# Weights in rings of fixed places, wide low parts and sums, and high products first, in a one-core transformer block

## The chip, the cores and the metric

The kernel runs on one core of a Trainium2 chip. The metric is the device time of one execution in microseconds. The time before is the median of three runs, and one more execution of the same program was profiled.

A core has a matrix engine (TensorE, PE in the profile; its loads of the stationary operand are shown apart as PEld), a vector engine (VectorE, DVE), a scalar engine (ScalarE, ACT), GpSimd (POOL), and a queue engine (SyncE, SP) that here issues most transfers. Each has its own queue of instructions. Data lie in SBUF, sums of products in PSUM, which here is used as eight banks of 128 rows by 512 float32 columns.

## The reference

One layer of a streaming encoder block, for 256 tokens (two blocks of 128 rows, `h` = 0 and 1 below) and a width of 4096, in float32:

```python
xn = rms_norm(h, norm_in_g[i])
proj = xn @ w_in[i]                       # 4096 x 14336
q, k, v, z_a, a_c, g_c, z_c = jnp.split(proj, ...)
y_a = chunked_attention(q, k, v, rel_table[i])
y_a = rms_norm(y_a, attn_out_g[i]) * silu(z_a)
y_c = conv_module(a_c, g_c, w_dw[i], b_dw[i], conv_ln_g[i], conv_ln_b[i], w_pw[i], b_pw[i])
y_c = rms_norm(y_c, conv_out_g[i]) * silu(z_c)
h = h + concatenate([y_a, y_c]) @ w_out[i]                    # 4096 x 4096
gate = sigmoid(rms_norm(h, ple_norm_g[i]) @ w_ple_gate[i] + b_ple_gate[i])   # 4096 x 4096
h = h + gate * (p[i] @ w_ple[i])
return rms_norm(h, final_g)
```

`conv_module` is a gated product, a causal depthwise convolution of 31 taps, a layer norm, a swish and a product with a 2048 x 2048 matrix (`w_pw`). Nearly all the arithmetic is in the products with the five weight matrices, each of which is read about once.

## The kernel before

**Products from high and low parts.** Each operand is split in two: a high part, rounded to the format in which TensorE multiplies fast (`F32R`), and a low part, which is what the rounding left. A product of two operands is three products of parts, called kinds: kind 0 is high left with high weight, kind 1 low left with high weight, kind 2 high left with low weight. The left operand (the activations, transposed) is the stationary one; the weights stream past it, 512 columns at a time. For a weight tile `wt`, `parts_of` (L199) writes the high part with a cast on ScalarE (L204) and the low part with a subtraction on VectorE (L205).

**Mixed products.** `mixed_product` (from L340) computes two blocks of 512 output columns for both row blocks: four sums, `c[h][j]`, in four PSUM banks of the pool `ps_acc`, which has just four. It goes through the contraction in pairs of row blocks of 128, in a given order (`dense`, `early` and so on, L329 to L338). An unmarked pair is a plain pair: for each of its two weight tiles of 128 x 1024 (`k` = 0 and 1), four banks by three kinds, 24 products (`add_plain`, L395). The banks have names: P2 is `c[0][0]`, P3 is `c[0][1]`, P4 is `c[1][0]`, X is `c[1][1]`. A pair marked `*` or `+` uses seven block products of three kinds in place of eight, 21 products, with sums of weight blocks (`ua`, `ub`) and four further banks P1, P5, P6 and P7 (`helper`, from `ps_tmp`). For `*` VectorE makes the sums (L465, L466, L472, L473); for `+` two of them are made by an accumulating transfer (`sums_ahead`, L404). Of the w0 tile only the first half needs parts in a seven.

**After a product.** When a mixed product is complete, its caller reads the four banks on VectorE, in the order of `QUARTERS`: c00, c10, c01, c11. These are called drains below: L535 in `scaled_pair`, L1028 and L1030 for the pointwise convolution, L1054 in `gated`, L1138 for `w_out`, L1180 for the gate. The next mixed product allocates the same four banks.

**Where the tiles lie.** Weight tiles come from the pool `wpool` with a buffer count for each tag: five for raw tiles (`w`), three each for high and low parts (`wh`, `wl`). The parts of the sums (`uh`, `ul`) have two each in `upool`. A new tile takes a buffer when all that touched the tile in it before are done.

**Order.** Instructions are traced in program order; a scheduler then fills each engine's queue, and can put an instruction that is ready ahead of an earlier one that isn't. `pin` keeps instructions in program order; it is used in the first pairs (`first_pairs`) and at the very end. `fill` takes small pieces of other work from the deque `later` (convolution taps, transposes' splits, gating) and issues them between pairs. `queued_behind` puts the sums' parts of a `+` pair behind the last recorded part instructions (`recent`).

**Stages.** Four gated products with the convolution (`glu_conv`), four for queries and keys (`keys`), one mixed product for values and two single ones (`single_values`, through `product`), attention after each group, two pointwise products, four for the gates z, four for `w_out`, four for the final gate with the embedding's products (`product` with `ps_tmp`). The last gate product holds three pairs back (`left`) and ends with pinned instructions.

The lines that the change touches: the pool (L73), the first tiles (L107), `weight_parts` and `part_tiles` (L187 to L197), `parts_of`, `add_plain`'s use in the loop (L432 to L450), the sums `ua` (L464 to L466) and the order of the seven (L482 to L488).

Of the kernel before, what the change touches and what calls it, by code (L numbers as in the profile page):

```python
# [10 lines left out]
F32 = mybir.dt.float32  # L11
# [14 lines left out]
def hybrid_block(  # L26
# [41 lines left out]
    def pool(name, bufs, stack=ctx, side=0, **kw):  # L68
        return stack.enter_context(tc.tile_pool(name=name, bufs=bufs, side=sides[side], **kw))

    cpool = pool("cpool", 1)
    act = pool("act", 8)
    wpool = pool("wpool", 5)  # L73
    big = pool("big", 8)
    keep = pool("keep", 1)
    ps_acc = pool("ps_acc", 4, space=bass.MemoryType.PSUM)
# [27 lines left out]
            ap=[list(rows.ap[0]), [apart, 2], [1, NB]],  # L104
        )

    w_first = [wpool.tile([P, 2, NB], F32, tag="w", name="wt") for _ in range(2)]  # L107
    for j, col in enumerate((o_a, o_g)):
        nc.scalar.dma_start(w_first[0][:, j], w_in0[:P, col : col + NB])
    for lo, hi in ((0, P), (P, 2 * P), (2 * P, NB)):  # L110
# [75 lines left out]

    def weight_parts(w, col, k0, kc, tiles=None):  # L187

        wt = wpool.tile([P, KC, NB], F32, tag="w", name="wt")
        nc.sync.dma_start(  # L190
            wt[:, :kc, :],
            w[k0 * P : (k0 + kc) * P, col : col + NB].rearrange("(k q) n -> q k n", q=P),
        )
        return parts_of(wt, kc, tiles)[0]

    def part_tiles():
        return [wpool.tile([P, KC, NB], F32R, tag=tag, name=tag, bufs=3) for tag in ("wh", "wl")]  # L197

    def parts_of(wt, kc, tiles=None):  # L199
        if tiles is None:  # L200
            tiles = part_tiles()
        wh, wl = tiles
        made = (
            nc.scalar.copy(wh[:, :kc, :], wt[:, :kc, :]),  # L204
            nc.vector.tensor_tensor(  # L205
                wl[:, :kc, :], wt[:, :kc, :], wh[:, :kc, :].bitcast(F32), ALU.subtract
            ),
        )
        recent[:] = made
        return (wh, wl), made  # L210

    recent = []

# [126 lines left out]
    def mixed_product(  # L340
# [54 lines left out]
        def add_plain(n, k, wh, wl, **kw):  # L395
            pair = order[n][0]
            for j in range(2):
                for h in range(NH):
                    name = (("P2", "P3"), ("P4", "X"))[h][j]
                    add(name, block(2 * pair + k, h), (wh[:, j], wl[:, j]), n, k == 1, **kw)  # L400

        sums = {}

        def sums_ahead(n):  # L404
# [22 lines left out]
        for n, (pair, seven) in enumerate(order):  # L427
            if n < done:
                continue
            if ahead:  # L430
                ahead(pair)
            wts = []  # L432
            for k in range(2):
                wt = wpool.tile([P, 2, NB], F32, tag="w", name="wt")
                if seven == "+" and k == 0:
                    nc.sync.dma_start(wt[:, 0], w[2 * pair * P : (2 * pair + 1) * P, col : col + NB])
                else:
                    nc.sync.dma_start(wt, two_columns(w, 2 * pair + k, col, apart))
                wts.append(wt)
            sums_ahead(n)  # L440
            if n >= len(order) - n_left:
                for k in range(2):
                    tiles = left[2 * (n - len(order) + n_left) + k]
                    held.append((2 * pair + k, parts_of(wts[k], 2, tiles and tiles())[0]))
                fill(fills[n % len(fills)])
                continue
            if not seven:
                for k in range(2):
                    add_plain(n, k, *parts_of(wts[k], 2)[0])
                fill(fills[n % len(fills)])  # L450
                continue
            begins = not helper
            if begins:
                for name in ("P1", "P5", "P7", "P6"):
                    helper[name] = ps_tmp.tile([P, NB], F32, tag="tmp", name=f"acc_{name}")
                banks.update(helper)
            w0, w1 = wts
            plus = partial(nc.vector.tensor_tensor, op=ALU.add)
            before = list(recent)
            w0h, w0l = parts_of(w0, 1)[0]  # L460
            if seven == "+":
                ua = ub = sums[n]
            else:
                ua = ub = upool.tile([P, 2, NB], F32, tag="u", name="ua")  # L464
                plus(ua[:, 0], w0[:, 0], w0[:, 1])  # L465
                plus(ua[:, 1], w0[:, 1], w1[:, 1])  # L466
            with queued_behind(before if seven == "+" else ()):
                uah, ual = pair_parts(ua)
            w1h, w1l = parts_of(w1, 2)[0]
            if seven == "*" and not sums:  # L470
                ub = upool.tile([P, 2, NB], F32, tag="u", name="ub")
            plus(ub[:, 0], ua[:, 0], w1[:, 1])  # L472
            plus(ub[:, 1], ub[:, 0], w1[:, 0])  # L473
            ubh, ubl = pair_parts(ub)
            first = len(made)

            def s_of(i):
                t, at = comb[pair] if isinstance(comb, dict) else (comb[pair // 4], pair % 4)
                return [t[:, at + i // 2, q, (i % 2) * P : (i % 2 + 1) * P] for q in range(2)]

            k0, k1 = 2 * pair, 2 * pair + 1
            add("P1", block(k0, 0), (w0h[:, 0], w0l[:, 0]), n, True)  # L482
            add("P5", s_of(1), (uah[:, 0], ual[:, 0]), n, True)
            add("P7", s_of(0), (uah[:, 1], ual[:, 1]), n, True)
            add("P2", block(k1, 0), (w1h[:, 0], w1l[:, 0]), n, True)
            add("P3", s_of(3), (w1h[:, 1], w1l[:, 1]), n, True)
            add("P6", s_of(2), (ubh[:, 0], ubl[:, 0]), n, True)
            add("P4", block(k1, 1), (ubh[:, 1], ubl[:, 1]), n, True)  # L488
            if begins and on_begin:
                on_begin()  # L490
            if begins:
                tc.add_manual_dep(
                    made[first].ins, last_transpose[0].ins.name,
                    mybir.DependencyInfo(mybir.DependencyClass.NoSync, mybir.DependencyReason.DATA),
                    reason="transposes before the helpers take their banks",
                )
            if n == last_seven:
                on_helpers(helper)
            fill(fills[n % len(fills)])
# [77 lines left out]
    def first_pairs(add):  # L577
# [5 lines left out]
        def load(n):  # L583

            weights.append([])
            for k in range(2):
                t = wpool.tile([P, 2, NB], F32, tag="w", name="wt")
                pin(nc.sync.dma_start(t, two_columns(w_in0, 2 * first[n][0] + k, o_a, o_g - o_a)))
                weights[n].append(t)
            if n < n_x:  # L590
                t = act.tile([P, NH, NB], F32, tag="act", name="xin")
                src = x[0, :, n * NB : (n + 1) * NB].rearrange("(h q) n -> q h n", q=P)
                pin(nc.sync.dma_start(t, src))
                xin.append(t)
# [625 lines left out]
    fill(len(later))  # L1220
    w_p = []
    for j in range(2):
        wt = wpool.tile([P, 2, NB], F32, tag="w", name="wt")
        nc.sync.dma_start(
            wt, w_ple[0, :, (c0 + j) * NB : (c0 + j + 1) * NB].rearrange("(k q) n -> q k n", q=P)
        )
        w_p.append(pair_parts(wt))
# [111 lines left out]
```

## Time and profile before

| | |
|---|---|
| median of 3 runs | 2034.01 us (2033.57 to 2034.16) |
| the profiled execution | 2032.83 us |
| span of its instructions | 2031.1 us |
| granted TensorE clock, mean | 0.998 |
| busy: PE, PEld, DVE, ACT | 99%, 82%, 92%, 59% |
| read from HBM | 430.77 MB, 214 GB/s over the span |

The profile gives, for each engine, the time in which it worked and, for idle time, which other instruction ended it. `L205` is line 205 of the kernel; a helper's line stands for all its callers, so rows are told apart by the names of the tiles. A row of the timeline is the start, the time from the first start to the last end of a run of like instructions, and their number. A matmul's own duration (0.39 us for 512 columns) is longer than the distance to the next one, since they overlap in the array.

### The profile page before, as it was taken

To read this page: it belongs to the slowest core of one execution; us is meant where nothing else is said; L and a number is where in the kernel's file an instruction comes from. 1 tells how busy PE (TensorE), PEld (TensorE's weight loads), DVE (VectorE), ACT (ScalarE), POOL (GpSimd) and SP (SyncE) were. 2 spreads that over 40 slices of the span, in tenths; PEclk is the share of its full clock that TensorE was granted. 3 is DMA by queue.
4 is the path that set the end of the run, shared out by engine and by line. 5 is a ranking of instruction groups with operands and counts; after the bars stand their busy time and mean duration, and the time that the engine had idled before them with its cause. 6 is when DMAs were issued, how large, how long until landed. Compare 5 with 4: busy or idle time off the path is not lost.

```text
span 2031.1 us, 26144 instructions
## 1 busy us (share of the span) xinstructions
PE 2015.5 (99%) x9094; PEld 1658.7 (82%) x9094; DVE 1871.1 (92%) x2658; ACT 1203.3 (59%) x1568; POOL 46.0 (2%) x50
## 2 busy tenths in 40 slices
PE   9999999999999999999999999999999999999997
PEld 7888888888888888888888888888888888888876
DVE  7999999679999986868899999999999999999998
ACT  7655555655655445676556566675665666665555
POOL 0000000000000000000000000000000000000000
PEclk9999999999999999999999999999999999999999
DMA  8787878688678867556666666676666656666765
GB/s 294 223 237 233 257 214 251 191 245 239 188 217 250 254 187 207 171 185 205 194 214 198 202 205 214 217 229 209 206 213 201 208 187 207 204 220 205 234 208 179
DMA packets 171167, 436.69 MB, mean 215 GB/s; under 512 B 13966, under 2 KB 17182, under 8 KB 171034
## 3 DMA queue, kind: packets, MB, share of 16 engines
q1 hardware_dynamic: 161952, 417.93, 64.0%
q0 software_dynamic: 8432, 16.25, 4.9%
q8 instruction: 71, 1.16, 0.2%
q10 hardware_dynamic: 650, 0.84, 0.1%
q14 instruction: 62, 0.51, 0.1%
HBM read 430.77 MB, written 4.19 MB: 214 GB/s over the span
## 4 chain that ended last, share of the span: by engine, by line
PE 92%; DVE 5%; issue 2%; ACT 1%; DMA 1%; POOLq 0%; POOL 0%; ACTq 0%; DVEq 0%
PE acc L383 67%; PE acc_P L383 16%; PE acc L229 5%; DVE wl L205 2%; PE tmp_ps L170 1%; DVE cv L721 1%; DMA wt<-in_w_out_dram 0%; PE tmp_ps L890 0%; DVE ul L205 0%; PE tmp_ps L874 0%; PE tmp_ps L908 0%; PE tmp_ps L913 0%; ACT wh L204 0%; PE acc L371 0%; DVE cv L799 0%
## 5 line engine op out<-in xcount | busy, mean ns | idle before, releaser
L383 PE MATMUL acc<-wh,big_t 128*128 128x512 f32 x3992 | 1234.7, 391 | 0.7 <-DVE y_c L1030 0.3
L204 ACT CAST wh<-wt 128x1024 fp32r<-128x1024 f32 (+1 forms) x737 | 713.4, 978 | 550.5 <-PE acc L383 365.0
L205 DVE TENSOR_TENSOR wl<-wt,wh 128x1024 fp32r<-128x1024 f32 (+1 forms) x737 | 821.8, 1127 | 82.0 <-ACT wh L204 78.6
L383 PEld LDWEIGHTS acc<-wh,big_t 128*128 128x128 f32 x3992 | 746.8, 188 | 155.1 <-issue 0.9
L383 PE MATMUL acc<-wl,big_t 128*128 128x512 f32 x1996 | 770.7, 391 | 0.6 <-DVE wl L205 0.5
L383 PEld LDWEIGHTS acc<-wl,big_t 128*128 128x128 f32 x1996 | 374.3, 188 | 79.5 <-DVE wl L205 2.3
L204 ACT CAST uh<-ua 128x1024 fp32r<-128x1024 f32 x160 | 168.3, 1052 | 80.9 <-DVE ua L466 46.1
L721 DVE SCALAR_TENSOR_TENSOR cv<-uT,dw,cv 128x250 f32<-128x250 f32 (+19 forms) x480 | 202.3, 463 | 1.1
L205 DVE TENSOR_TENSOR ul<-ua,uh 128x1024 fp32r<-128x1024 f32 x160 | 194.9, 1218 | 8.4 <-ACT uh L204 8.0
L383 PE MATMUL acc_P<-uh,big_t 128*128 128x512 f32 x516 | 157.9, 391 | 0.0
L204 ACT CAST uh<-ub 128x1024 fp32r<-128x1024 f32 x92 | 96.8, 1053 | 95.8 <-DVE ub L473 86.5
L205 DVE TENSOR_TENSOR ul<-ub,uh 128x1024 fp32r<-128x1024 f32 x92 | 112.2, 1220 | 6.1 <-ACT uh L204 5.2
L383 PEld LDWEIGHTS acc_P<-uh,big_t 128*128 128x128 f32 x516 | 95.8, 188 | 22.3 <-ACT uh L204 3.1
L383 PE MATMUL acc_P<-ul,big_t 128*128 128x512 f32 x258 | 98.8, 391 | 0.1
L229 PE MATMUL acc<-wh,big_t 128*128 128x512 f32 x304 | 93.9, 390 | 0.0
L465 DVE TENSOR_TENSOR ua<-wt 128x512 f32<-128x512 f32 x95 | 65.1, 685 | 18.3 <-DMA wt<-in_w_in_dram 12.4
L383 PE MATMUL acc<-uh,big_t 128*128 128x512 f32 x252 | 78.1, 390 | 0.0
L383 PE MATMUL acc_P<-wh,big_t 128*128 128x512 f32 x252 | 77.8, 389 | 0.0
L229 PEld LDWEIGHTS acc<-wh,big_t 128*128 128x128 f32 x304 | 56.9, 188 | 11.9 <-issue 0.2
L383 PE MATMUL acc_P<-uh,comb_t 128*128 128x512 f32 x216 | 66.4, 390 | 0.1
L466 DVE TENSOR_TENSOR ua<-wt 128x512 f32<-128x512 f32 x95 | 64.9, 683 | 1.1 <-DMA wt<-in_w_in_dram 1.1
L473 DVE TENSOR_TENSOR ub<-ub,wt 128x512 f32<-128x512 f32 x92 | 63.0, 685 | 0.8
(250 smaller groups left out, 1589.3 us busy)
## 6 DMA issues: line engine op xcount, KB each, us to landing
wt<-in_w_in_dram SPq DMA_DIRECT2D x416, 512.0 KB, 4.5
wt<-in_w_out_dram SPq DMA_DIRECT2D x128, 512.0 KB, 4.3
wt<-in_w_ple_gate_dram SPq DMA_DIRECT2D x128, 512.0 KB, 4.2
wt<-in_w_pw_dram SPq DMA_DIRECT2D x32, 512.0 KB, 4.7
ua<-in_w_in_dram SPq DMA_DIRECT2D x31, 512.0 KB, 4.2
ua<-in_w_in_dram POOLq DMA_DIRECT2D x31, 512.0 KB, 8.3
wt<-in_w_in_dram SPq DMA_DIRECT2D x31, 256.0 KB, 2.7
hc<-in_x_dram SPq DMA_DIRECT2D x8, 512.0 KB, 4.8
```

The costliest lines, as they stand in the source:

```text
L170: nc.tensor.transpose(pt[:, i * T + h * P : i * T + (h + 1) * P], src[:, h, b] if len(src.shape) == 4 else src[:, h, b * P : (b + 1) * P], ...
L204: nc.scalar.copy(wh[:, :kc, :], wt[:, :kc, :]),
L205: nc.vector.tensor_tensor(wl[:, :kc, :], wt[:, :kc, :], wh[:, :kc, :].bitcast(F32), ALU.subtract),
L229: nc.tensor.matmul(acc, a, b[:, k, :], start=kb == 0 and kind == 0, stop=kb == kblocks - 1 and kind == 2,)
L383: nc.tensor.matmul(banks[name], a, b, start=name not in begun, stop=final and ends[name] == n and kind == 2 and not (left and name in "P2 ...
L465: plus(ua[:, 0], w0[:, 0], w0[:, 1])
L466: plus(ua[:, 1], w0[:, 1], w1[:, 1])
L473: plus(ub[:, 1], ub[:, 0], w1[:, 0])
L721: nc.vector.scalar_tensor_tensor(cv[:, i, PAD - k :], uT[:, i, : T + k - PAD], dw[:, b, k : k + 1], cv[:, i, PAD - k :], ALU.mult, ALU.add,)
```

## The change

Raw weight tiles and their parts no longer come from pool buffers but from three tiles that hold them all: five raw places, three high and three low. A counter hands out places in turn. Since the two tiles of a plain pair now lie in one tile, a strided view takes both (`places`; where the ring wraps, its step is negative), and one VectorE instruction of 128 x 2048 writes both low parts, after two casts. In a seven whose sums VectorE makes, `ua`'s two halves come from one instruction: w0's first half and w1's second half, each plus w0's second half, which is read twice by a broadcast view. In a plain pair, kinds 0 and 1 of both tiles go first, then kind 2 of both; the bank changes faster than the left operand does. In a seven, kinds 0 and 1 of the products with raw blocks, then those with `ua`, then kind 2 of each, then P6 and P4 as before. Orders, fills, casts, transfers and the number of products stay the same.

```diff
-    wpool = pool("wpool", 5)
+    wpool = pool("wpool", 1)
...
-    w_first = [wpool.tile([P, 2, NB], F32, tag="w", name="wt") for _ in range(2)]
+    RAW, PARTS = 5, 3
+    w_ring = wpool.tile([P, RAW, 2, NB], F32, name="wt")
+    wh_ring, wl_ring = (wpool.tile([P, PARTS, 2, NB], F32R, name=name) for name in ("wh", "wl"))
+    taken = {RAW: 0, PARTS: 0}
+
+    def place(n):
+
+        taken[n] += 1
+        return (taken[n] - 1) % n
+
+    def raw_place():
+        return w_ring[:, place(RAW)]
+
+    def places(n, of):
+
+        return slice(of[0], of[-1] + 1) if of[-1] > of[0] else slice(of[0], None, of[-1] - of[0])
+
+    w_first = [raw_place() for _ in range(2)]
...
     def part_tiles():
-        return [wpool.tile([P, KC, NB], F32R, tag=tag, name=tag, bufs=3) for tag in ("wh", "wl")]
+        at = place(PARTS)
+        return wh_ring[:, at], wl_ring[:, at]
...
+    def parts_of_pair(raw):
+
+        at = [place(PARTS) for _ in range(2)]
+        halves = [(wh_ring[:, i], wl_ring[:, i]) for i in at]
+        casts = [nc.scalar.copy(wh, w_ring[:, i]) for (wh, _), i in zip(halves, raw)]
+        src, to = places(RAW, raw), places(PARTS, at)
+        low = nc.vector.tensor_tensor(
+            wl_ring[:, to].rearrange("q k j n -> q k (j n)"),
+            w_ring[:, src].rearrange("q k j n -> q k (j n)"),
+            wh_ring[:, to].rearrange("q k j n -> q k (j n)").bitcast(F32), ALU.subtract,
+        )
+        recent[:] = *casts, low
+        return halves
...
+        def add_pair(n, parts):
+
+            pair = order[n][0]
+            for kinds in ((0, 1), (2,)):
+                for k, (wh, wl) in enumerate(parts):
+                    for h in range(NH):
+                        for kind in kinds:
+                            for j in range(2):
+                                name = (("P2", "P3"), ("P4", "X"))[h][j]
+                                add(name, block(2 * pair + k, h), (wh[:, j], wl[:, j]), n, k == 1, (kind,))
...
             if not seven:
-                for k in range(2):
-                    add_plain(n, k, *parts_of(wts[k], 2)[0])
+                add_pair(n, parts_of_pair(raw_at))
...
-                plus(ua[:, 0], w0[:, 0], w0[:, 1])
-                plus(ua[:, 1], w0[:, 1], w1[:, 1])
+                blocks = w_ring.rearrange("q k j n -> q (k j) n")
+                a, d = 2 * raw_at[0], 2 * raw_at[1] + 1
+                plus(
+                    ua, blocks[:, a : d + 1 : d - a] if d > a else blocks[:, a : d - 1 if d else None : d - a],
+                    blocks[:, a + 1 : a + 2].broadcast_to([P, 2, NB]),
+                )
...
-            add("P1", block(k0, 0), (w0h[:, 0], w0l[:, 0]), n, True)
-            add("P5", s_of(1), (uah[:, 0], ual[:, 0]), n, True)
-            add("P7", s_of(0), (uah[:, 1], ual[:, 1]), n, True)
-            add("P2", block(k1, 0), (w1h[:, 0], w1l[:, 0]), n, True)
-            add("P3", s_of(3), (w1h[:, 1], w1l[:, 1]), n, True)
+            raw = (
+                ("P1", block(k0, 0), (w0h[:, 0], w0l[:, 0])),
+                ("P2", block(k1, 0), (w1h[:, 0], w1l[:, 0])),
+                ("P3", s_of(3), (w1h[:, 1], w1l[:, 1])),
+            )
+            two = (
+                ("P5", s_of(1), (uah[:, 0], ual[:, 0])),
+                ("P7", s_of(0), (uah[:, 1], ual[:, 1])),
+            )
+            for group, kinds in ((raw, (0, 1)), (two, (0, 1)), (raw, (2,)), (two, (2,))):
+                for product_of in group:
+                    add(*product_of, n, True, kinds)
             add("P6", s_of(2), (ubh[:, 0], ubl[:, 0]), n, True)
             add("P4", block(k1, 1), (ubh[:, 1], ubl[:, 1]), n, True)
```

More of the change, by code (lines that the diff above doesn't have):

```diff
@@ L187, in weight_parts @@
     def weight_parts(w, col, k0, kc, tiles=None):
-        wt = wpool.tile([P, KC, NB], F32, tag="w", name="wt")
+        wt = raw_place()
         nc.sync.dma_start(
@@ L431, in mixed_product @@
                 ahead(pair)
-            wts = []
+            wts, raw_at = [], []
             for k in range(2):
-                wt = wpool.tile([P, 2, NB], F32, tag="w", name="wt")
+                raw_at.append(place(RAW))
+                wt = w_ring[:, raw_at[k]]
                 if seven == "+" and k == 0:
@@ L586, in load @@
             for k in range(2):
-                t = wpool.tile([P, 2, NB], F32, tag="w", name="wt")
+                t = raw_place()
                 pin(nc.sync.dma_start(t, two_columns(w_in0, 2 * first[n][0] + k, o_a, o_g - o_a)))
@@ L1222, in hybrid_block @@
     for j in range(2):
-        wt = wpool.tile([P, 2, NB], F32, tag="w", name="wt")
+        wt = raw_place()
         nc.sync.dma_start(
```

## The prediction

> **What bounds the kernel now.** I read the page first (busy times, the chain of waits), then the busy time by stretch, then the longest pieces of the chain, and last the timeline where one product ends and the next begins.
>
> ```profile
> span 2031.1 us, 26144 instructions
> PE 2015.5 (99%) x9094; PEld 1658.7 (82%) x9094; DVE 1871.1 (92%) x2658; ACT 1203.3 (59%) x1568; POOL 46.0 (2%) x50
> PE 92%; DVE 5%; issue 2%; ACT 1%; DMA 1%; POOLq 0%; POOL 0%; ACTq 0%; DVEq 0%
> ```
>
> In the view by stretch the columns are the stretch, its length, then busy time of PE, PEld, DVE, ACT and POOL, the granted clock, and DMA:
>
> ```profile
> 1143.00:1225.00 82.00, 82.00 (x363) 67.70 (x362) 78.31 (x94) 49.33 (x55) 0.00 (x0) 1.00 0.64 206
> 2000.00:2031.00 31.00, 18.44 (x97) 15.82 (x97) 21.90 (x40) 12.96 (x25) 1.86 (x2) 0.87 0.44 160
> ```
>
> TensorE is idle for 2031.1 - 2015.5 = 15.6 us, and 31.00 - 18.44 = 12.6 of these lie in the last stretch, where the output is scaled and stored. That leaves 3.0 us of visible idle time in the 2000 us before. A busy matmul here means one in the pipe, so I also take the spacing from two unbroken pieces of the chain:
>
> ```profile
> 713.29 43.57 PE acc L229 x192
> 1143.11 17.17 PE acc L383 x75
> ```
>
> 43.57 / 192 = 0.2269 us for one product. (17.17 / 75 gives 0.2289, with one or two short breaks in it.) A plain pair of row blocks is 24 products, 24 x 0.2269 = 5.4 us; a pair in the seven-product form is 21, 4.8 us. TensorE runs at this spacing nearly everywhere. The change issues no fewer products, so work saved on VectorE is worth at most the few stalls that are left, while each new stall is paid in full.
>
> **VectorE's saving, off the path.** Two low parts of 1024 columns become one of 2048, in plain pairs; two sums of 512 become one of 1024, in sevens whose sums are not fetched by DMA.
>
> ```profile
> L205 DVE TENSOR_TENSOR wl<-wt,wh 128x1024 fp32r<-128x1024 f32 x611 | 738.2, 1218 | 82.0 <-ACT wh L204 78.6 <-PE tmp_ps L170 1.5
> L465 DVE TENSOR_TENSOR ua<-wt 128x512 f32<-128x512 f32 x95 | 65.1, 685 | 18.3 <-DMA wt<-in_w_in_dram 12.4 <-DMA wt<-in_w_out_dram 4.4 <-DMA wt<-in_w_ple_gate_dram 1.2
> ```
>
> Of the 611 low parts 126 belong to sevens (one per seven; the orders have 126), 32 to the two single value products, 16 to the pinned start, 6 to the embedding and 3 to the end: 428 are left, 214 plain pairs. The sums give 95 sevens. What one instruction fewer saves is read from starts, since neighbours overlap:
>
> ```profile
> 1083.91 0.68 DVE L465 TENSOR_TENSOR ua<-wt 128x512 f32<-128x512 f32 x1
> 1084.51 0.68 DVE L466 TENSOR_TENSOR ua<-wt 128x512 f32<-128x512 f32 x1
> ...
> 1090.45 2.35 DVE L205 TENSOR_TENSOR wl<-wt,wh 128x1024 fp32r<-128x1024 f32 x2
> 1092.72 0.68 DVE L466 TENSOR_TENSOR ua<-wt 128x512 f32<-128x512 f32 x1
> ```
>
> 512 columns take 0.60 from start to start, 1024 take (1092.72 - 1090.45) / 2 = 1.135; the fixed part is 2 x 0.60 - 1.135 = 0.065 us, so the wide low part should take 2 x 1.135 - 0.065 = 2.20. The saving is (214 + 95) x 0.065 = 20 us of VectorE's 1871, all of it beside TensorE's products: nothing on the path. Its bounds are 0 and the 3.0 us of idle time above.
>
> **High products first inside a product.** A plain pair asked for its first low part at the third product; now it asks at the 17th, 16 x 0.227 = 3.6 us in. The casts alone start it. Against that, the wide low part waits for both casts and for both of its places, and a place is read later: the 20th product of the pair before, where it was the 12th. So its time runs from about 0.7 us before the pair to 3.6 us into it, 4.3 us for 2.2 us of work: it fits, unless something stands in front of it in VectorE's queue. A stall such as this one should then shrink:
>
> ```profile
> 838.51 1.98 PE L383 MATMUL acc<-wh,big_t 128*128 128x512 f32 x8
> 839.75 2.35 DVE L205 TENSOR_TENSOR wl<-wt,wh 128x1024 fp32r<-128x1024 f32 x2
> 841.01 1.20 PE L383 MATMUL acc<-wl,big_t 128*128 128x512 f32 x4 [0.53 <-DVE wl L205]
> ```
>
> Bounds 0 to -3.0; I take -1.2, under half, as some of these waits are on sums. In a seven, w0's low place is held to the 11th product, not the 3rd, but its low part is also wanted only then: nothing, and a rival below if that fails. A raw place frees about 1.1 us later, since both wait for the wide instruction; the load that follows lands in 4.5 us and has a pair and a half of lead, over 7 us: nothing.
>
> ```profile
> wt<-in_w_in_dram SPq DMA_DIRECT2D x416, 512.0 KB, 4.5
> ```
>
> **The end of a product, on the path.** This is what I think decides. Every mixed product fills four PSUM banks, and the next one takes the same four. Before, the last pair goes bank by bank, so the first bank is complete nine products before the end:
>
> ```profile
> 96.54 0.39 PE L383 MATMUL acc<-wl,big_t 128*128 128x512 f32 x1
> 97.05 2.78 DVE L535 SCALAR_TENSOR_TENSOR z<-acc,r_x,z 128x512 f32<-128x512 f32 x4 [1.35 <-PE acc L383]
> ...
> 98.58 0.39 PE L383 MATMUL acc<-wl,big_t 128*128 128x512 f32 x1
> 98.81 0.61 PE L383 MATMUL acc<-wh,big_t 128*128 128x512 f32 x2
> ```
>
> The first bank's last product starts at 96.54, VectorE (which waits for it) begins to drain at 97.05, 0.51 later, and the next product begins at 98.81 with no pause. How soon it could begin after a drain is seen at two ends where the drain was late:
>
> ```profile
> 988.57 0.68 DVE L1030 TENSOR_TENSOR y_c<-acc,row 128x512 f32<-128x512 f32 x1
> 989.17 1.21 DVE L205 TENSOR_TENSOR wl<-wt,wh 128x1024 fp32r<-128x1024 f32 x1
> 990.30 1.88 DVE L1030 TENSOR_TENSOR y_c<-acc,row 128x512 f32<-128x512 f32 x3
> 990.32 0.39 PE L383 MATMUL acc<-wl,big_t 128*128 128x512 f32 x1
> 991.04 0.73 PE L383 MATMUL acc<-wh,big_t 128*128 128x512 f32 x2 [0.33 <-DVE y_c L1030]
> ```
>
> ```profile
> 1071.99 2.47 DVE L1054 TENSOR_TENSOR z<-acc,z 128x512 f32<-128x512 f32 x4
> 1072.22 0.39 PE L383 MATMUL acc<-wl,big_t 128*128 128x512 f32 x1
> 1072.82 0.70 PE L383 MATMUL acc<-wh,big_t 128*128 128x512 f32 x2 [0.21 <-DVE z L1054]
> ```
>
> 991.04 - 990.30 = 0.74 and 1072.82 - 1071.99 = 0.83 from a drain's start to the first product in that bank. So the first bank needs 0.51 + 0.74 = 1.25 to 1.34 us between its last product and its next first; before, it had ten spacings, 2.27. In the new order the last pair's last eight products are the low ones, k by k, and each bank ends among the last four: the first has four spacings, 0.91 us. The next product starts 0.34 to 0.43 late, and a broken run costs 0.08 to 0.11 more (two products in 0.70 and 0.73, against 0.62): 0.48 a time, if VectorE is free. The other three drains follow at 0.60 each and TensorE has four ready products per free bank, 0.91, so they add nothing if it takes them bank by bank.
>
> VectorE is often not free. The place that the next pair's wide low part needs comes free with the 20th product, one ahead of the first bank's last. If VectorE sits idle at that moment the low part goes in front of all four drains, as one did at 989.17: 2.20 - 0.23 more, 2.45 in all. Both bounds are kept; taking the low part in front one time in five, 0.8 x 0.48 + 0.2 x 2.45 = 0.9 us.
>
> How many ends? Four drains each:
>
> ```profile
> L535 DVE SCALAR_TENSOR_TENSOR z<-acc,r_x,z 128x512 f32<-128x512 f32 x36 | 24.9, 744 | 2.7 <-PE acc L383 2.7
> L1138 DVE TENSOR_TENSOR hc<-acc,hc 128x512 f32<-128x512 f32 x16 | 10.4, 683 | 0.0
> L1054 DVE TENSOR_TENSOR z<-acc,z 128x512 f32<-128x512 f32 x16 | 10.1, 680 | 0.0
> L1180 DVE SCALAR_TENSOR_TENSOR z<-acc,r_h,z 128x512 f32<-128x512 f32 x12 | 8.2, 741 | 0.4 <-PE acc L383 0.4
> ```
>
> 9 + 4 + 4 + 3, and two of the pointwise products: 22. Some are covered by other work for TensorE:
>
> ```profile
> 355.98 0.38 PE L889 MATMUL tmp_ps<-kT,qT 128*128 128x128 f32 x2
> ...
> 1320.81 1.36 PE L170 MATMUL tmp_ps<-ident,qT 128*128 128x128 f32 x11
> ...
> 1747.15 0.61 PE L229 MATMUL acc<-wh,big_t 128*128 128x512 f32 x2
> ```
>
> Attention (three ends), the transposes before w_out and before the gate (two), the embedding's 24 products after each of three gates. 22 - 8 = 14 ends, 14 x 0.9 = 12.6 us (6.7 to 34.3). The stalls of 991.04 (0.49) and 1072.82 (0.37), 0.9 in all, are inside the old time and come off.
>
> **The sum.** The profiled execution took 2032.83, 1.2 under the median of the three runs, 2034.01. 2032.83 + 12.6 - 0.9 - 1.2 = 2043.3, on the median's footing 2044.5 us.
>
> **Rivals.**
>
> The order covers the ends: 2031 to 2035, say 2032.5. The rows from 838.51 show that TensorE's order isn't the program's: eight products with high parts ran in a row while low parts were missing. Should the order that is built let the first bank's low products go early, so that its last is at least six from the end (1.34 / 0.227), the ends cost nothing and only the gain of up to 3.0 us remains. Against it: at 96.54 to 98.81 all operands were there and the order was the program's.
>
> Neighbours with the same stationary operand run closer, faster than before. In a plain pair each left operand now serves two products in a row; 214 x 12 = 2568 products follow one with the same operand. What a product costs beside its columns:
>
> ```profile
> L383 PE MATMUL acc<-wh,big_t 128*128 128x512 f32 x3992 | 1234.7, 391 | 0.7 <-DVE y_c L1030 0.3 <-DVE z L1054 0.2
> L371 PE MATMUL part<-big_t 128*128 128x256 f32 x18 | 2.5, 283 | 0.0
> L125 PEld LDWEIGHTS <-idle x10: 102/151/151, 1.2 to 5.4; 128*128 128x128 bf16 x10
> ```
>
> 256 columns more take 391 - 283 = 108 ns, so 512 take 216 of the 227: 11 ns, 2568 x 11 = 28 us, 2006. It decides if the operand isn't loaded again. Against it: the ten warm-up products use one operand, and all ten loaded it; the page counts 9094 loads for 9094 products. The Trainium skill ("TensorE: Matmul & The Clock Gate", Step-by-step) says weights typically stay put so that one load serves many matmuls; its Back-to-back issue gap gives about 216 ns for 512 columns, which would make the same 28 us; the trace's loads speak against it here.
>
> Sevens starve: places are held longer and the one sum waits for both raw tiles. The row of L465 has 18.3 us of waits for tiles in 95 sevens, 0.2 each. If TensorE lost that much at each of 126 sevens and broke a run (0.1): 126 x 0.3 = 38 more, 2082. Against it, the later need.
>
> Waits go by the stretch from the first to the last place, not by place. When a pair's raw tiles lie in places 4 and 0, one pair in five, the loads into 1 to 3 would wait for its low part: it ends 1.5 us into the pair, the loads land 4.5 later and the cast takes 1.0, 7.0 against a pair of 5.4, 1.6 us late. With (214 + 126) / 5 = 68 such pairs, 109 us: 2143.
>
> **Chances.** Ends of products as worked out 0.54 (own range 2038 to 2060); covered ends 0.27; same operand 0.07; starving sevens 0.07; whole stretches 0.05. About 0.2%, 4 us, is what a measurement of this kernel can tell from no change. Faster: 0.07 and 0.05 of the covered case; the same: 0.22; slower: 0.54 + 0.07 + 0.05. The range takes all but the far rivals: from 2031 (covered ends) to 2068 (2034 + 34.3, every end at its upper bound).
>
> **What would show it.** Right: TensorE idle grows from 3.0 us before the last stretch to some 10, in breaks at the ends of products, with drains (L535, L1054, L1138 of before) named; the first product of the next follows the first drain by 0.74 to 0.83; VectorE's busy time falls some 40 us. Wrong: ends without breaks; a spacing other than 0.227; PEld under the count of PE; breaks at every seven; loads that wait for low parts.

## The result, and the profile after

The changed kernel takes 2114.82 us (median of six), the kernel before 2034.09 us beside it. The ratio is 1.0392, 95% interval 1.0372 to 1.0412: 81 us slower. One of the six executions took 3431.65 us at a granted clock of 0.555 and is left out of the ratio; the other five took 2109.0 to 2119.41. The execution profiled took 2119.41.

First the page of the kernel after: span, busy times, and the chain of waits by engine.

```profile
span 2117.6 us, 25737 instructions
PE 2045.7 (97%) x9094; PEld 1660.4 (78%) x9094; DVE 1858.3 (88%) x2349; ACT 1198.1 (57%) x1568; POOL 50.4 (2%) x50
PE 39%; DVE 8%; issue 3%; DMA 2%; ACT 2%; ACTq 0%; POOLq 0%; POOL 0%; DVEq 0%; SPq 0%
```

The products are as many as before, 9094, each still with its own load of the stationary operand. VectorE does less (1858.3 against 1871.1). TensorE's idle time went from 15.6 to 2117.6 - 2045.7 = 71.9 us, and the chain of waits, which was 92% PE, now changes engine often: its shares add up to 54% only, since it could be followed back through about half of the span, and PE has 39 of these 54. The same stretch of time as before, by windows (by then the kernel after is some 47 us behind, but both are among the like products for the gates z; stretch, length, busy PE, PEld, DVE, ACT, POOL, granted clock, DMA):

```profile
1143.00:1225.00 82.00, 79.79 (x349) 64.45 (x348) 74.43 (x76) 46.56 (x53) 0.00 (x0) 1.00 0.61 199
```

349 products where there were 363. At the same clock, that is 14 x 0.2269 = 3.2 us lost in 82. What TensorE waited for (view of waits: total us, times, longest):

```profile
PE acc_P L415 <- ACT uh L222: 14.4, 19, 3.0
PE acc L415 <- DVE z L589: 11.7, 5, 3.2
PE acc_P L415 <- DVE ul L223: 8.9, 12, 1.4
PE acc L415 <- DVE hc L1192: 5.6, 5, 1.7
PE tmp_ps L928 <- DVE z L589: 5.4, 3, 2.6
PE acc L415 <- DVE z L1108: 5.0, 3, 1.7
PE acc L415 <- DVE wl L236: 2.3, 5, 0.8
```

There are two kinds: drains of the four banks (z, hc; L589, L1192 and L1108 are L535, L1138 and L1054 of before), and the parts of the sums in sevens (uh, ul). The low parts of plain pairs themselves are hardly waited for.

These rows count only time in which no matmul is in the pipe. For the comparisons below I took the starts of all matmuls and added up what lies between two of them beyond the spacing. A break here is more than 0.25 us; it goes to the end of a product, or to the part that the next matmul reads. An end counts as such when the next matmul waited for a drain. "Rest" is everything smaller, restarts and products at a low clock included. In us, of each profiled execution:

| | ends | uh, ul | wl | wh | rest |
|---|---|---|---|---|---|
| before | 1.1 | 0.3 | 0.7 | 0 | 19.7 |
| after | 33.8 (20 breaks) | 28.7 (32 breaks) | 3.9 | 1.6 | 37.2 |

**An end of a product**, in the timeline of after (start, length, engine, operation, count; in brackets the idle time before it):

```profile
1552.67 1.98 PE L415 MATMUL acc<-wl,big_t 128*128 128x512 f32 x8
1553.83 2.29 DVE L236 TENSOR_TENSOR wl<-wt,wh 128x2048 fp32r<-128x2048 f32 x1 [1.87 <-ACT wh L222]
1554.48 0.61 PE L415 MATMUL acc_P<-wh,big_t 128*128 128x512 f32 x2
1556.04 2.48 DVE L1192 TENSOR_TENSOR hc<-acc,hc 128x512 f32<-128x512 f32 x4
1556.78 3.93 PE L415 MATMUL acc<-wh,big_t 128*128 128x512 f32 x16 [1.68 <-DVE hc L1192]
```

The eight low products run in their order (7 spacings in 1.98 - 0.39, 0.227 each). VectorE, idle for 1.87 us, takes the wide low part 0.2 us before the first bank is complete, and all four drains stand behind it. (The profile names a cast as what ended the idle time, but that cast had ended 0.22 us earlier; the fourth of the eight low products, the last to read the place that the low part needs, ended at 1553.35 + 0.39 = 1553.74; that is 0.09 us before the wide part starts.) The next product starts 0.74 us after the first drain. The wide part stood directly ahead of the drains at 14 of the 22 ends; these make 30.6 of the 33.8 us, 1.84 to 3.33 us each. They are nearly the 14 that the prediction called uncovered. But one of them is the end that attention was to cover (the row at 355.98 in the prediction), which lost 1.89, and at the first end of the pointwise product, an uncovered one, no wide part stood in front.

**Sevens**, two pieces of the same timeline:

```profile
1067.31 1.23 DVE L510 TENSOR_TENSOR ua<-wt 128x1024 f32<-128x1024 f32 x1 [0.66 <-DMA wt<-in_w_in_dram]
1068.45 2.29 DVE L236 TENSOR_TENSOR wl<-wt,wh 128x2048 fp32r<-128x2048 f32 x1
1068.82 1.98 PE L415 MATMUL acc<-wh,big_t 128*128 128x512 f32 x8
1070.65 1.22 DVE L223 TENSOR_TENSOR ul<-ub,uh 128x1024 fp32r<-128x1024 f32 x1
1071.93 0.50 PE L415 MATMUL acc_P<-ul,big_t 128*128 128x512 f32 x1 [1.13 <-DVE ul L223]
```

```profile
142.02 0.34 SPq L480 DMA_DIRECT2D wt<-in_w_in_dram  x1
143.01 2.28 DVE L236 TENSOR_TENSOR wl<-wt,wh 128x2048 fp32r<-128x2048 f32 x1
143.21 0.39 PE L415 MATMUL acc<-wh,big_t 128*128 128x512 f32 x1
144.50 1.04 ACT L234 CAST wh<-wt 128x1024 fp32r<-128x1024 f32 x1 [2.98 <-DMA wt<-in_w_in_dram]
145.45 1.04 ACT L222 CAST uh<-ua 128x1024 fp32r<-128x1024 f32 x1
146.55 1.16 PE L415 MATMUL acc_P<-uh,comb_t 128*128 128x512 f32 x2 [2.95 <-ACT uh L222]
```

In the first, `ul` of a seven stands behind the wide low part of a later pair, which in turn stands behind a sum that had waited 0.66 us for a raw tile. In the second, ScalarE waits 2.98 us for a raw tile, its cast of `uh` stands behind that, and TensorE waits 2.95.

### The profile page after: what moved, and what is told of

Read it like the earlier page. It is cut to its first block, busy times and chain, and to the rows that moved or that the text cites. A ratio compares the mean times of both kernels' runs of the same rounds, so it can differ in the third digit from the quotient of the medians.

```text
span 2117.6 us, 25737 instructions
## 1 busy us (share of the span) xinstructions
PE 2045.7 (97%) x9094; PEld 1660.4 (78%) x9094; DVE 1858.3 (88%) x2349; ACT 1198.1 (57%) x1568; POOL 50.4 (2%) x50
## 4 chain that ended last, share of the span: by engine, by line
PE 39%; DVE 8%; issue 3%; DMA 2%; ACT 2%; ACTq 0%; POOLq 0%; POOL 0%; DVEq 0%; SPq 0%
PE acc L415 29%; PE acc_P L415 8%; DVE wl L236 2%; DVE ul L223 2%; DMA wt<-in_w_ple_gate_dram 1%; DVE wl L223 1%; ACT uh L222 1%; PE acc L261 1%; PE tmp_ps L187 0%; DVE ub L520 0%; DVE ua L510 0%; DMA wt<-in_w_in_dram 0%; ACT wh L222 0%; DVE ub L519 0%; DMA wt<-in_w_out_dram 0%
## 5 line engine op out<-in xcount | busy, mean ns | idle before, releaser
L415 PE MATMUL acc<-wh,big_t 128*128 128x512 f32 x3992 | 1008.4, 394 | 24.9 <-DVE z L589 11.7
L415 PEld LDWEIGHTS acc<-wh,big_t 128*128 128x128 f32 x3992 | 750.2, 189 | 189.3 <-issue 14.6
L234 ACT CAST wh<-wt 128x1024 fp32r<-128x1024 f32 x428 | 447.5, 1051 | 343.7 <-PE acc L415 230.0
L236 DVE TENSOR_TENSOR wl<-wt,wh 128x2048 fp32r<-128x2048 f32 x214 | 489.5, 2287 | 127.9 <-PE acc L415 80.0
L415 PE MATMUL acc<-wl,big_t 128*128 128x512 f32 x1996 | 526.4, 391 | 2.8 <-DVE wl L236 2.3
L222 ACT CAST wh<-wt 128x1024 fp32r<-128x1024 f32 (+1 forms) x309 | 270.1, 876 | 339.4 <-PE acc L415 233.3
L223 DVE TENSOR_TENSOR wl<-wt,wh 128x1024 fp32r<-128x1024 f32 (+1 forms) x309 | 308.0, 1002 | 20.3 <-ACT wh L222 14.5
L775 DVE SCALAR_TENSOR_TENSOR cv<-uT,dw,cv 128x232 f32<-128x232 f32 (+26 forms) x480 | 199.5, 463 | 0.7
L510 DVE TENSOR_TENSOR ua<-wt 128x1024 f32<-128x1024 f32 x95 | 116.0, 1221 | 24.0 <-DMA wt<-in_w_out_dram 13.0
L415 PEld LDWEIGHTS acc_P<-uh,big_t 128*128 128x128 f32 x516 | 94.9, 188 | 34.1 <-ACT uh L222 15.6
L261 PE MATMUL acc<-wh,big_t 128*128 128x512 f32 x304 | 94.0, 390 | 0.4 <-DVE z L589 0.4
L415 PEld LDWEIGHTS acc_P<-ul,big_t 128*128 128x128 f32 x258 | 48.4, 188 | 23.7 <-DVE ul L223 13.9
```

The lines of the kernel that those rows point to most:

```text
L223: nc.vector.tensor_tensor(wl[:, :kc, :], wt[:, :kc, :], wh[:, :kc, :].bitcast(F32), ALU.subtract),
L234: casts = [nc.scalar.copy(wh, w_ring[:, i]) for (wh, _), i in zip(halves, raw)]
L236: low = nc.vector.tensor_tensor(wl_ring[:, to].rearrange("q k j n -> q k (j n)"), w_ring[:, src].rearrange("q k j n -> q k (j n)"), wh_rin ...
L261: nc.tensor.matmul(acc, a, b[:, k, :], start=kb == 0 and kind == 0, stop=kb == kblocks - 1 and kind == 2,)
L415: nc.tensor.matmul(banks[name], a, b, start=name not in begun, stop=final and ends[name] == n and kind == 2 and not (left and name in "P2 ...
L510: plus(ua, blocks[:, a : d + 1 : d - a] if d > a else blocks[:, a : d - 1 if d else None : d - a], blocks[:, a + 1 : a + 2].broadcast_to([ ...
```

## The experiments

In each diff, lines with a minus are those of the kernel named. All were timed beside the kernel before, which took 2033.2 to 2033.6 us (medians) in these sessions.

### What does each part cost?

**The orders alone.** The kernel before with `add_pair` and the new order in sevens; pool buffers, narrow low parts and narrow sums stay.

```diff
-                for k in range(2):
-                    add_plain(n, k, *parts_of(wts[k], 2)[0])
+                add_pair(n, [parts_of(wts[k], 2)[0] for k in range(2)])
...
+            for group, kinds in ((raw, (0, 1)), (two, (0, 1)), (raw, (2,)), (two, (2,))):
```

> The kernel before with the new orders of products alone: pools, narrow low parts and narrow sums as before. Ends theory: each bank ends among the last four products, so at 14 ends 0.5 to 1.6 us are lost (one narrow part in front at most): 2041 to 2056, with breaks at the ends and nearly none at sevens. If rings and wide instructions make all of the loss: 2034.

2063.58 us, ratio 1.0140 (1.0124 to 1.0155), 30 us slower and above what was expected; breaks in us: ends 15.0, wl 6.8, wh 3.2, uh and ul 1.2.

**The rings alone.** The kernel after with the low parts, the sums and both orders of before:

```diff
-                add_pair(n, parts_of_pair(raw_at))
+                for k in range(2):
+                    add_plain(n, k, *parts_of(wts[k], 2)[0])
...
+                plus(ua[:, 0], w0[:, 0], w0[:, 1])
+                plus(ua[:, 1], w0[:, 1], w1[:, 1])
```

> The kernel before with its tiles in rings of places and nothing else (narrow low parts, narrow sums, old orders). Theory (rings cost nothing by themselves: waits go by place, a place frees in the order in which the buffers did): 2032 to 2037. Rival (waits go by the stretch from first to last place, or a strict turn of places is dearer than any free buffer): over 2045.

2033.94 us, ratio 1.0003 (0.9994 to 1.0012). Rings cost nothing. No instruction of this run takes two places at once, so it can't tell whether such a view makes waits go by the stretch between its places. The trace of the kernel after can, with the places counted in the order of the loads: 46 of the 214 pairs lie in places 4 and 0, and the loads into 1, 2 and 3 were issued before the end of the wide low part at all of them but two (the third load), as with the other pairs. The two loads into its own places are issued 0.0 and 0.5 us behind its end (medians). So waits go by place, not by stretch, and both raw places are held until the joint low part is done.

**The wide sums alone**, on the rings: the `plus` over a broadcast view of the change, nothing else.

> Rings and the wide first sums alone: narrow low parts, old orders. One sum of 1.22 us for two of 0.68 saves 0.065 us of VectorE in 95 sevens and waits for both raw tiles. Theory (it is beside TensorE's products, and the sums are wanted late): 2030 to 2036. If the wait for both tiles starves sevens: 2045 or more.

2035.82 us, ratio 1.0012 (1.0003 to 1.0022), some 2 us.

**The wide low part alone**, on the rings, in the old orders:

```diff
-                for k in range(2):
-                    add_plain(n, k, *parts_of(wts[k], 2)[0])
+                for k, both in enumerate(parts_of_pair(raw_at)):
+                    add_plain(n, k, *both)
```

> Rings and the wide low part of a plain pair alone: old orders, narrow sums. Theory (the wide part is long and stands in front of others, and in the old order it is wanted at the third product): 2060 to 2110, with breaks before products with wl and before those with uh or ul, and none over 0.6 us at the ends. If the wide part costs only through the late ends of the banks: 2034 to 2040.

2080.94 us, ratio 1.0234 (1.0219 to 1.025), 47 us slower. In the old order the first low product is the third of a pair, and TensorE waits for it; the rows of its waits (PEld's are those of the loads of the stationary operand, which can wait beneath a running product; breaks at low parts come to 26.6 us):

```profile
PEld acc L415 <- DVE wl L236: 53.0, 91, 3.1
PE acc L415 <- DVE wl L236: 22.2, 23, 2.7
```

So the two large parts, each alone, are the wide low part (47) and the orders (30). That 47 + 30 is close to 81 doesn't show that they add up, since they lose at different places alone and together: the wide part loses at the third product in the old order, and at ends and sevens in the new one.

**The new order in sevens, with wide sums**, on the rings, with the old order and narrow low parts in plain pairs:

> Rings, wide sums and the new order of the seven, with the plain pairs as before (bank by bank, narrow low parts). Both new orders alone measured 2063.6, of which 15.4 us were breaks at the ends and 7 before low parts. If the plain pairs' order makes that loss: 2031 to 2038. If the seven's order has a good share: 2045 or more.

2034.53 us, ratio 1.0006 (0.9996 to 1.0015). With narrow low parts the order in sevens costs nothing. The kernel of 2053.8 us below has the plain pair's new order besides, so on rings, with narrow low parts, that order costs 2053.8 - 2034.5 = 19.3 us. What made 30 of it on pool buffers with narrow sums is not shown.

**The old order in sevens**, all else as after:

```diff
-            for group, kinds in ((raw, (0, 1)), (two, (0, 1)), (raw, (2,)), (two, (2,))):
-                for product_of in group:
-                    add(*product_of, n, True, kinds)
+            add("P1", block(k0, 0), (w0h[:, 0], w0l[:, 0]), n, True)
+            add("P5", s_of(1), (uah[:, 0], ual[:, 0]), n, True)
...
```

> The changed kernel with the seven products of a seven in the order of before (each product's three kinds together). In the changed kernel's profile TensorE loses some 35 us inside products, before products with uh or ul. If the new order of the seven makes them: 2080 or less. If they come from the wide low part standing in front of the parts of the sums on VectorE, and from later loads: unchanged or slower, 2105 to 2130.

2094.39 us, ratio 1.0297 (1.028 to 1.0314). That is 20 us less than after, between the two ranges: uh and ul fell from 28.7 to 11.0. The order that costs nothing beside narrow low parts costs 20 us beside wide ones, so it sharpens the wide part's fault and has none of its own that shows.

### The ends

**The last pair of each product bank by bank**, all else as after:

```diff
-                add_pair(n, parts_of_pair(raw_at))
+                parts = parts_of_pair(raw_at)
+                if n < len(order) - 1:
+                    add_pair(n, parts)
+                else:
+                    for k, both in enumerate(parts):
+                        add_plain(n, k, *both)
```

> The changed kernel, but the last pair of each mixed product goes bank by bank as before (both low parts still in one wide instruction). Ends theory (in the profile of the changed kernel 14 of 22 ends have the wide low part directly in front of the four drains, and TensorE waits 1.84 to 2.45 us at 12 of them, 30 us over all ends, besides the slower clock after such waits): the first bank is complete nine products before the end, so the drains go first; some 30 to 38 us come back: 2075 to 2085, and no break over 0.6 us at an end. Rival (the wide instruction is in front of whatever is urgent, wherever the banks end): under 10 us come back, 2105 or more, and the breaks stay.

2092.76 us, ratio 1.0292 (1.0276 to 1.0307). The breaks at ends went from 33.8 to 1.7; the time fell by 22 us only, outside the range. The waits show what came instead: in the last pairs a low part is asked for at the third product again. Breaks at low parts rose from 3.9 to 18.2 us, over half of them inside last pairs.

```profile
PE acc L415 <- DVE wl L236: 12.3, 12, 3.0
PE acc_P L415 <- ACT uh L222: 11.4, 19, 2.6
```

**Two narrow low parts for each pair**, all else as after:

```diff
-        low = nc.vector.tensor_tensor(
-            wl_ring[:, to].rearrange("q k j n -> q k (j n)"),
...
+        lows = [
+            nc.vector.tensor_tensor(wl, w_ring[:, i], wh.bitcast(F32), ALU.subtract)
+            for (wh, wl), i in zip(halves, raw)
+        ]
```

> The changed kernel with two low parts of 1024 columns per plain pair in place of the wide one; order of products, rings and wide sums stay. Ends theory: at each end a drain waits behind at most one narrow part, 1.1 us less, 14 x 1.1 = 15 us back, and a like share of the waits at sevens: 2085 to 2100. If the width is all that matters: 2040 or less. If the order alone makes the stalls: 2110 or more.

2053.8 us, ratio 1.0100 (1.0085 to 1.0115): 61 us less than after, far more than I had expected. Ends fell to 16.1, uh and ul to 2.2. The wide low part is behind nearly all of the breaks in sevens and over half of those at ends. The largest row of ends, and that of `uh`, in TensorE's waits:

```profile
PE acc L414 <- DVE z L588: 5.9, 5, 1.7
PE acc_P L414 <- ACT uh L222: 0.5, 2, 0.3
```

**Both of these**: narrow low parts, and the last pair bank by bank.

> Rings, wide sums and the new orders, with narrow low parts and the last pair of each product bank by bank. Theory: the wide low part and the banks' late end are the two causes; with narrow lows alone 2053.8 us were measured, with 16.1 us of breaks at the ends, and these go: 2034 to 2040, breaks at the ends under 2 us. If something else in the rings or the orders costs: 2045 or more.

2041.36 us, ratio 1.0040 (1.0025 to 1.0055), just above the range. Ends 2.7 (under 2 was expected), uh and ul 2.8. Here only the last pair changes against the run before, so the order at the ends costs 2053.8 - 2041.36 = 12.4 us where low parts are narrow, and the breaks at ends differ by 16.1 - 2.7 = 13.4.

### Why the wide low part costs 61 us: its length, or its joint wait?

**Two instructions of 1024 columns, each over the same half of both tiles.** Each is as short as a narrow low part, but still waits for both casts and both places, and holds both raw tiles until it is done.

```diff
-        low = nc.vector.tensor_tensor(
-            wl_ring[:, to].rearrange("q k j n -> q k (j n)"),
...
+        lows = [
+            nc.vector.tensor_tensor(
+                wl_ring[:, to, j], w_ring[:, src, j], wh_ring[:, to, j].bitcast(F32), ALU.subtract
+            )
+            for j in range(2)
+        ]
```

> The changed kernel with its wide low part cut in two another way: two instructions of 1024 columns, each over the same half of both tiles, so that each still waits for both casts and both places, as the wide one does, but none is longer than 1.22 us. Measured so far: wide 2114.8, two narrow ones (one tile each) 2053.8. If the length of one instruction in front of urgent ones is the cause: within 15 us of 2053.8, 2040 to 2069. If the wait for both casts and both places is the cause: over 2095. Between them both count, by where it falls.

2098.93 us, ratio 1.0317 (1.0302 to 1.0333). The ends are those of narrow low parts, 15.3 against 16.1; uh and ul are those of after, 28.6 against 28.7. The length is worth 2114.8 - 2098.9 = 16 us and lies at the ends (33.8 against 15.3); the joint wait is worth 2098.9 - 2053.8 = 45 us, and its breaks are in the sevens. The theory that the length decides has fallen. TensorE's waits in front of the sums' parts here:

```profile
PE acc_P L416 <- ACT uh L222: 21.4, 19, 3.2
PE acc_P L416 <- DVE ul L223: 2.4, 5, 0.5
```

VectorE's groups (busy, mean ns | idle before, by releaser), first of this kernel, then of the one with narrow low parts, then one more row of the latter's waits:

```profile
L237 DVE TENSOR_TENSOR wl<-wt,wh 128x1024 fp32r<-128x1024 f32 x428 | 510.5, 1220 | 119.3 <-ACT wh L222 51.9 <-ACT wh L234 33.7 <-PE acc L416 20.0
```

```profile
L237 DVE TENSOR_TENSOR wl<-wt,wh 128x1024 fp32r<-128x1024 f32 x428 | 515.2, 1223 | 81.2 <-ACT wh L222 25.3 <-PE acc L414 24.2 <-issue 13.8
```

```profile
DVE wl L237 <- ACT wh L234: 12.5, 13, 2.4
```

As many instructions of one length, but the time in which VectorE stands at one of them for a cast grew from 25.3 + 12.5 = 38 to 51.9 + 33.7 = 86 us.

**Four low places instead of three** (and, to make room, four raw places instead of five), else as after.

> The changed kernel with four places for low parts and, to make room, four for raw tiles in place of five. A pair's low places are then those of two pairs earlier, so the wide part needn't wait for the pair before. In the changed kernel VectorE sits idle for 80 us before wide low parts until TensorE has read a place. If this wait at the head of VectorE's queue makes a good part of the loss: 2060 to 2095, and that idle time under 20 us. If the length of the instruction alone does it: 2105 or more; if the lost raw place costs, slower than 2125.

2109.73 us, ratio 1.0376 (1.0359 to 1.0394), in the range given for the length alone, which the run above rules out. VectorE's idle time ahead of the low parts is no longer for places but for casts:

```profile
DVE wl L239 <- ACT wh L237: 118.3, 85, 4.2
```

This run can't tell how much of the joint wait is for low places, since it has a raw place less, and the last run shows what that costs.

**Four raw places with narrow low parts**: the kernel of 2053.8 us with one number changed.

```diff
-    RAW, PARTS = 5, 3
+    RAW, PARTS = 4, 3
```

> The kernel after with two narrow low parts for each plain pair measured 2053.8 us with five places for raw tiles; here there are four, and nothing else differs. Theory that raw tiles arriving late starve the sevens (the casts that wait for a load: 1.3 us before, some 39 us in the kernel after, some 70 us with the low part cut into halves of both tiles): with a place less the loads start later, 2070 to 2100 us, TensorE's breaks in front of the uh and ul products at 10 us or more (2.2 us with five places), casts waiting for loads above 30 us. Rival, that the raw places have slack and the joint wait for both casts alone starves the sevens: at most 2060 us, and those breaks below 6 us.

2088.99 us, ratio 1.0273 (1.0255 to 1.029): 35 us for one raw place, with breaks at uh and ul of 17.9 (2.2 with five) and no wide instruction. The casts of raw tiles wait 110 us for loads, 8 with five places; the three largest rows with four:

```profile
ACT wh L234 <- DMA wt<-in_w_in_dram: 37.7, 35, 5.5
ACT wh L222 <- DMA wt<-in_w_ple_gate_dram: 31.7, 19, 4.0
ACT wh L222 <- DMA wt<-in_w_in_dram: 22.7, 13, 3.8
```

In the kernel after these waits come to 39 us, before to 1.3; the largest row of after, and the only one of before:

```profile
ACT wh L234 <- DMA wt<-in_w_in_dram: 18.6, 16, 3.9
```

```profile
ACT wh L204 <- DMA wt<-in_w_in_dram: 1.3, 1, 1.3
```

So raw places have no slack in the new orders, and late tiles alone are enough to give breaks in the sevens. The joint low part holds w0's place until w1's cast is done. Followed back through the waits of ScalarE and VectorE, as the profile infers them, the breaks in front of uh and ul lead to a load that had not landed: 27.6 of 28.6 us with halves, 24.2 of 28.7 after, 16.7 of 17.9 in the last run. How much such a late tile costs depends on what stands behind it in the queues: with 39 us of late loads after loses 28.7 in these breaks, with 110 the last run loses 17.9. How the 45 us divide between the two is left open; a sixth raw place would tell, and was not tried.

One change at a time, the loss adds up: 2034.5 with rings, wide sums and the new sevens; 19.3 for the plain pair's order (2053.8); 45.1 for the joint low part in halves (2098.9); 15.9 for one wide instruction (2114.8). No version run here beats the kernel before; the nearest leave the plain pair as it was.

## Why the prediction was wrong, point by point

The sign was right, the size not: 2044.5 was forecast, with a range to 2068, and 2114.8 measured.

**What bounds the kernel: right.** TensorE's products set the time, the spacing stayed 0.227, and each new stall was paid in full.

**VectorE's saving, off the path: right in place, high in size.** The wide low part takes 2.20 us from start to start, as worked out (1068.45 to 1070.65). VectorE's busy time fell by 12.8 us, not 20, and the "some 40" among the signs was a sum of durations that overlap in the busy time. None of it reached the end.

**"It fits, unless something stands in front of it": the gain did not come.** The window of 4.3 us was worked out for a plain pair that follows a plain pair. For the plain pairs' own low parts it nearly held, but the saving of 1.2 us was a loss: breaks at low parts went from 0.7 to 3.9 us (6.8 with the orders alone). The plain pair's order itself costs 19.3 us on rings, where breaks at ends are 16.1; the larger loss of the orders alone, 30, was not taken apart further.

**The end of a product: mechanism right, share wrong.** First drain to first product was to be 0.74 to 0.83: 0.74 in the rows above, up to 0.89 at the drains of L589. An end behind a wide low part was to lose 2.45: 1.84 (L1192, L1108) to 3.33 (L589) were measured, 2.2 in the mean. The step that failed is "one time in five": it was 14 ends, nearly all of the uncovered ones. The rows I quoted held the reason, since a place read to the 20th product comes free one product ahead of the first bank: the low part is ready first each time that VectorE is idle, and it was idle for 1.87 us and more ahead of 11 of these 14. 33.8 us at ends are just under the upper bound of 34.3, where 12.6 was taken; with narrow low parts and the last pair undone the order at ends is worth 12.4.

**"In a seven … nothing" and "a raw place frees about 1.1 us later … nothing": failed, and the largest error.** Breaks in front of uh and ul came to 28.7 us. The 1.1 us counted the length of the wide instruction and not its wait for the second cast. Measured from the end of w0's cast to the end of the low part that frees its place, it is 7.6 us after, 7.7 with halves and 3.5 with two narrow low parts (means of 214 pairs), so w0's place frees 4.1 us later; the casts then wait 39 us for loads, 1.3 before. I weighed the later place against one load's lead, without asking what stands behind a low part that waits: on VectorE the sums and their low parts, on ScalarE, behind a cast that waits for its tile, the cast of uh. With narrow low parts these breaks are 2.2 us. The rival of starving sevens named this and the sum of 38 for it; it got 0.07, from the later need of w0's low part, when the parts of the sums were what came late.

**What was not counted: the rest.** Shorter breaks, restarts and slow products grew from 19.7 to 37.2 us. About 9 of that is the clock (last section).

**The other rivals fell.** Covered ends: every uncovered end broke. Whole stretches: the loads into the places between did not wait (see the run of the rings alone). The same stationary operand: PEld x9094 beside PE x9094, so each product still loads its own, and the spacing stayed 0.227. The rule of the Trainium skill that stood beside it ("TensorE: Matmul & The Clock Gate", Step-by-step), one load for many products, did not come about by order alone.

## What to carry to other kernels

Merging two instructions saves the fixed part of one (here 0.065 us) and makes the first half wait for the second half's operands, and the second half's buffers wait with it. Count what stands behind that wait in the engine's queue, as `ul` stood behind the wide low part here and the cast of `uh` behind a cast that waited 2.98 us. Where the merged instruction was there to spread work ahead of a bottleneck, the price is paid there: 45 us of joint waiting against 12.8 us less work on an engine that was not the bound. And an order that completes all accumulators at once needs the drains to be first in the queue; what became ready just before them was ahead of them here at 14 of 22 ends, not at one in five.

## What the hardware showed that I had not expected

TensorE runs at half its clock for some microseconds after some of the long waits. The windows of the kernel after, around a wait of 3.17 us at an end (columns as above):

```profile
97.00:100.00 3.00, 3.00 (x15) 2.40 (x13) 0.00 (x0) 0.72 (x1) 0.36 (x1) 1.00 1.05 357
100.00:103.50 3.50, 0.33 (x3) 0.07 (x1) 3.14 (x3) 1.38 (x2) 0.87 (x1) 0.82 0.84 197
103.50:108.50 5.00, 5.00 (x12) 3.94 (x13) 3.14 (x5) 1.26 (x2) 0.00 (x0) 0.50 0.78 224
```

```profile
103.46 5.83 PE L415 MATMUL acc<-wh,big_t 128*128 128x512 f32 x13 [3.17 <-DVE z L589]
```

Granted clock 0.50; products at a spacing near 0.427 until it is given back, 12 of them here. Six of the eight breaks of 2.3 us and more in this profile were followed by 3 to 12 such products, 44 in all, 44 x (0.427 - 0.227) = 8.8 us on top of the waits; breaks of 2.36 and 2.45 us were followed by none. The Trainium skill ("TensorE: Matmul & The Clock Gate", What's actually happening) gives one idle window of about 3.4 us for this; here two breaks of 2.45 us were enough and a third was not.
